# A planned single-core mixer layer: new projection order, longer holds for side matmuls, later landing times, and ScalarE as a second engine for three scalings

## The chip, the cores and the metric

The kernel runs on one core of a Trainium2 chip. The metric is the device time of one execution in microseconds (us); the median of several executions counts. The core has a matrix engine (TensorE, PE in the profile), a vector engine (VectorE, DVE), an activation engine (ScalarE, ACT), GpSimd (POOL), and queues that start transfers (DMA), nearly all of them here on SyncE (SP).

## The reference

One layer of a streaming encoder, with D = 2048 channels and 512 frames. Two groups of heads read the same projection of the input, RWKV-7 (8 pairs of heads of 64 channels) and HGRN2 (8 heads of 128 channels). Their gated results go through one output projection and a LayerNorm.

```python
proj = einsum('btd,dc->btc', x, w_in)                 # 2048 -> 8320 columns
rw, hg = token_shift(proj[..., :4224], mu), proj[..., 4224:]
r, k, v, z, wd, ad = split(rw)                        # RWKV-7
decay = exp(-exp(-softplus(-(w0 + tanh(wd) @ w_up)) - 0.5))
a = sigmoid(a0 + ad @ a_up)
kk = normalized(k * k_k);  k = k * (1 + (a - 1) * k_a)
S = S * decay + (S @ -kk) (kk * a)^T + v k^T;  o = S r    # per frame and head
o_rwkv = (groupnorm(o) + sum(r * k * r_k) * v) * silu(z)
q, f, i, g = split(hg)                                # HGRN2
f' = lb + (1 - lb) * sigmoid(f);  k' = (1 - lb) * sigmoid(-f)
S = S * f' + k' i^T;  o = silu(q) S                       # per frame and head
o_hgrn = rmsnorm(o) * g_norm_w * silu(g)
y = concat(o_rwkv, o_hgrn) @ w_out
out = layer_norm(2**0.25 * x + y, ln_w, ln_b)
```

## The kernel before

**Main matmuls.** Every fp32 operand of a projection is split into a high and a low part (`split`, one ScalarE copy and one VectorE subtraction per 128x512 part), and a product is three matmuls: high by high, high by low, low by high (`three`, L524 in the profile). The input projection is a list of units, `ORDER`: `k3` is the key projection of RWKV head pair 3, `f6` the forget gate of HGRN head 6, and so on. A unit is 48 such matmuls of 128x512 (an `i` unit 192). `ORDER` also sets the layout of the weights in memory. The output projection follows: one quarter of the columns directly (`rows`), half of them by seven Strassen products of 8 blocks, the last quarter directly, with the LayerNorm at the end.

**Side matmuls.** The recurrences run in chunks between the main matmuls. Each head pair gets ready after its `k` and `r` (`rwkv_prep`), is transposed through DRAM (`rwkv_turn`, which waits for `v`), its 64x64 systems are inverted (`rwkv_invert`, two batches of 32x32 matmuls per two pairs) and folded (`folded`, two batches of 64x64), then a scan of 8 chunks with whole-array 128x128 fp32 matmuls (`rwkv_scan`), outputs, group norm, the gate. HGRN heads go in twos (`hgrn_heads`, `hgrn_out`). Matmuls with fewer than 128 rows or columns are called narrow, 128x128 fp32 ones whole; a stretch of side matmuls between two main ones is a visit.

**The planner.** The program is written out once, by a planner (`Plan`) that keeps a clock for every engine. Every piece of side work is a generator in a queue; after each main matmul `pump` issues what fits. An instruction's place in its engine's stream is thus fixed when the program is made, by costs written in the source; the chip then only obeys semaphores. What matters here:

- `three` adds n/2400 + 0.0145 us per main matmul to PE's clock, and `TURN` = 0.215 us at each change between whole-array and narrow modes.
- `worth`: a side matmul that is ready waits until another queue has one of its kind (whole or narrow) ready as well, or until `HOLD` is over (0.3 us for whole, 1.0 for narrow). This doesn't hold in the last six projections (`HURRY`), nor when PE is already on a visit. `BURST` limits narrow matmuls to 68 in 3 us.
- `step`: a PE instruction is issued only if its operands are ready 0.35 us before now (`LEAD`); another engine's when it can start soon.
- `fetched`: a load is taken to land at its transfer time (bytes at 360 GB/s) + 1.8 us after SP's clock; `send` adds 0.44 us to SP's clock, and does not look at whether the source or the destination is ready. SP executes its transfers in order: one that waits holds back those behind it.
- `Op` has one or more engines that could do it; `best` takes the one that would end first. `ts` (a scale, or a scale and an offset per channel) has VectorE alone.

The steps that the change touches: `gates` (two scalings per HGRN head), `rwkv_prep` (the key factor `a`), `put_gated` (a finished gated block is written to DRAM, and its partner is read back for sums that Strassen needs), `reload` (gated blocks read back for the output projection), `load` (weights), `finish_last` and `row_last` with its helper `biased` (the last 128 rows: eight matmuls without a use stand between the bias product and the mean product).

Of the kernel before, what the change touches and what calls it, by code (L numbers as in the profile page):

```python
# [10 lines left out]
AF = mybir.ActivationFunctionType  # L11
ALU = mybir.AluOpType
# [4 lines left out]
T = 512  # L17
# [14 lines left out]
HALF = 1024  # L32
# [7 lines left out]
ORDER = (  # L40
# [3 lines left out]


ORDER = (
# [3 lines left out]


def _order():

    return [(u[0], int(u[1:])) for u in ORDER.split()]
# [10 lines left out]
class Plan:  # L65
# [4 lines left out]

    AFTER = {"pe": 0.2, "act": 0.145, "dve": 0.13, "pool": 0.06, "dma": 0.0, None: 0.1}
    TO_PE = 0.12
    HOLD = {"whole": 0.3, "narrow": 1.0}
    TURN = 0.215
    REST = 1.5
    LEAD = -0.35
# [81 lines left out]
            self.short.pop(0)  # L158
        return not self.short or len(self.short) + n <= self.BURST

    def fetched(self, tile, size):

        self.clock["dma"] = max(self.clock["dma"], self.clock["sp"]) + size * 128 / 360e3
        self.ready[tile.tensor.name] = (self.clock["dma"] + 1.8, "dma")

    def queue(self):
        self.queues.append([])
# [95 lines left out]
def mixer_kernel(ctx, tc, head, x_r, w_all, par, up, ln_wb, consts, hmask, out):  # L263
    nc = tc.nc
    pe, sc_e, dve, pool = nc.tensor, nc.scalar, nc.vector, nc.gpsimd
# [17 lines left out]
    plan = Plan({**BUFS, **PBUFS})  # L283
# [26 lines left out]
    def room(**need):  # L310

        return lambda: all(plan.free(tag, n) for tag, n in need.items())
# [17 lines left out]
    def send(o, i, cost=0.44):  # L330

        nc.sync.dma_start(o, i)  # L332
        plan.clock["sp"] = max(plan.clock["sp"], plan.clock["pe"]) + cost


    def size(ap):
        n = 1
        for s in ap.shape[1:]:
            n *= s
        return n  # L340
# [23 lines left out]
    def act_way(o, i, f, scale=1.0, bias=0.0):  # L364
        cost = 0.09 + size(o) * 0.00085 + moved(o, i) + (0.06 if isinstance(scale, bass.AP) else 0.0)
        if f == AF.Copy:
            return "act", cost, lambda: sc_e.activation(o, i, f, scale=scale)  # L367
        return "act", cost, lambda: sc_e.activation(o, i, f, scale=scale, bias=bias)  # L368
# [4 lines left out]
    def dve_op(reads, o, f, n=None, per=0.00104, base=0.07):  # L373
        return Op([("dve", base + (n or size(o)) * per, f)], reads, [o])
# [5 lines left out]
    def banked(ap):  # L380

        return 0.00104 if ap.tensor.name in plan.banks else 0.00076

    def ts(o, a, s1, s2, f1, f2=None):
        if f2 is None:
            return dve_op([a], o, lambda: dve.tensor_scalar(o, a, s1, None, f1), per=banked(a))
        return dve_op([a], o, lambda: dve.tensor_scalar(o, a, s1, s2, f1, f2), per=banked(a))

    def stt(o, a, s, b, f1, f2):
        return dve_op([a, b], o, lambda: dve.scalar_tensor_tensor(o, a, s, b, f1, f2), per=0.00113,  # L390
# [72 lines left out]
    nhead = 2 * FIRST  # L463
# [21 lines left out]
    def load(j):  # L485
        if j < nload:
            if j < joint or (j - joint) % 4 < 2:
                t = st("wr", [P, HALF])
                raws[j] = [t[:, :QT], t[:, QT:]]
                send(t, source(j))  # L490
                plan.fetched(t, 4 * HALF)
            else:
                raws[j] = third[(j - joint) % 4 - 2]
                for i, t in enumerate(raws[j]):
                    send(t, source(j)[:, i * QT : i * QT + QT])
                    plan.fetched(t, 4 * QT)
# [22 lines left out]
    def three(ps, lh, ll, rh, rl, first, last):  # L519
        n = size(rh)  # L520
        for i, (l, r) in enumerate(((lh, rh), (lh, rl), (ll, rh))):
            plan.clock["pe"] += n / 2400 + 0.0145 + plan.turn(("main",))
            plan.mode = ("main",)
            pe.matmul(ps, l, r, start=first and i == 0, stop=last and i == 2)  # L524
            plan.pump()
        if last:
            plan.ready[ps.tensor.name] = plan.busy[ps.tensor.name] = (plan.clock["pe"], "pe")
# [85 lines left out]
    olb, lbm = lw[:, 4], lw[:, 5]  # L613

    HW0, HA0, HKA, HRK, HGW, HGB, HHW, HOKA = range(8)

    def hcol(i, p):

        return half[:, i, p : p + 1]
# [53 lines left out]
    gated = [None] * KT  # L673
# [3 lines left out]
    spilled, stored = {}, []  # L677
# [10 lines left out]
    def put_gated(k, g):  # L688

        gated[k] = g  # L690
        if k in SPILL:
            def run():
                yield lambda: by_now(g)
                send(spill[SPILL.index(k)], g)
                now = spilled[k] = plan.clock["sp"]
                n = korder.index(k)
                m, other = n // 2, korder[n ^ 1]
                if other in spilled:
                    yield room(t=1)
                    r = take("t")  # L700
                    send(r, spill[SPILL.index(other)])
                    plan.fetched(r, 4 * T)
                    yield lambda: plan.clock["pe"] > now + 4.5
                    r1, r2 = (r, g) if n % 2 else (g, r)
                    yield from token_sums(r1, r2, r1, r2)
                    for i, r_ in enumerate((r1, r2)):
                        yield lambda: by_now(r_) and plan.clock["sp"] <= plan.clock["pe"] + 0.2
                        send(sums_a[m, i], r_)
                    stored.append(m)
                    drop(r)  # L710
                drop(g)

            plan.add(stores, run())
# [31 lines left out]
    def rwkv_prep(S, p):  # L745
# [7 lines left out]
        a, sg, kx2 = take("t"), take("t"), take("t")  # L753
# [55 lines left out]
        yield tt(ar[:, :, :C], chunks(kap), pf[:, :, :C])  # L809
        yield stt(kap, a, 1.0, kap, ALU.add, ALU.mult)  # L810
        yield stt(bk[:, :, :C], chunks(kap), 0.5, chunks(pinv), ALU.mult, ALU.mult)
        yield ts(a, a, hcol(HKA, p), hcol(HOKA, p), ALU.mult, ALU.add)
        yield tt(k, k, a)
        yield tt(bk[:, :, C:], chunks(k), chunks(pinv))
        drop(a, kap, pinv)
# [480 lines left out]
    def gates(ps, h, put):  # L1296

        def run():
            yield evac_room(2)
            f, k = take("t"), take("t")  # L1300
            yield act(f, ps, AF.Sigmoid)
            yield act(k, ps, AF.Sigmoid, scale=-1.0)
            drop(ps)
            yield ts(f, f, olb[:, h : h + 1], lbm[:, h : h + 1], ALU.mult, ALU.add)
            yield ts(k, k, olb[:, h : h + 1], None, ALU.mult)
            put(f, k)

        plan.add(evacs, run())
# [137 lines left out]
    def reload(n):  # L1446
        while len(asked) < min(n, KT):
            k = korder[len(asked)]
            asked.append(k)
            if k in SPILL:  # L1450
                plan.until(lambda: gated[k] is not None and (plan.free("t") or plan.free("g")))
                gated[k] = take("t" if plan.free("t") else "g")
                send(gated[k], spill[SPILL.index(k)])
                plan.fetched(gated[k], 4 * T)

    def split_gated(n):
        while len(whole) < min(n, KT):
# [483 lines left out]
    def row_last(t, d, ps, halves):  # L1941

        y, k = place(t, d)

        def run():
            yield lambda: (t, d) in xrs
            xr = xrs[t, d]
            yield keyed(stt(y, xr, ALPHA, ps, ALU.mult, ALU.add), [xr.tensor.name, ps.tensor.name], k + [y.tensor.name])
            drop(ps, xr)
            for i in range(2):  # L1950
                yield lambda: len(halves) > i
                c = slice(i * T // 2, i * T // 2 + T // 2)
                kc = y_keys(t, d * T + c.start, d * T + c.stop)
                yc, pc = y[:, c], halves[i]

                def weigh():
                    w = lnw[0][:, 0, d * T + c.start : d * T + c.stop]
                    yield keyed(tt(yc, yc, w), kc, kc)

                yield keyed(tt(yc, yc, pc, ALU.add), kc + [pc.tensor.name], kc)  # L1960
                yield keyed(Op([("dve", 0.07 + T // 2 * 0.00105,
                                 lambda: dve.bn_stats(stats[:, t, d + i], yc))], [], []), kc, [f"stat{t}"])
                if i == 1:

                    yield room(mix=2)
                    pbs = {e: take("mix") for e in (2, 3)}
                    plan.add(scans[1], biased(pbs))
                    yield from finish_last(t, pbs, weigh)
                    return
                yield from weigh()  # L1970

        def biased(pbs):
            for e in (2, 3):
                yield mm(pbs[e], ident, columns(t, e)[2], stop=False)
            warm = take("main" if plan.free("main") else "mix")
            for _ in range(8):
                pe.matmul(warm, gh[0][:, :P], gl[0])
                plan.clock["pe"] += 0.2275
            drop(warm)

        plan.add(sums, run())
# [132 lines left out]
```

## Time and profile before

| | us |
|---|---|
| three runs | 1018.35, 1015.20, 1016.61 |
| median | 1016.61 |
| the profiled execution | 1017.52 |
| its span, first to last instruction | 1015.7 |
| first main matmul of the output projection | 829.7 |
| VectorE busy | 864.3 |
| ScalarE busy | 507.5 |

The profiled execution is 0.9 us above the median; 1.8 us of it lie outside the span. The page gives busy time by engine; PE's is nearly the whole span because the matmuls overlap in the pipeline, so it doesn't tell how much of it is waiting. That is read from three other views: the table of waits, the chain of work that ended last (each step with what released it), and the timeline (instructions by start). There a row has the start, the time taken, the engine, the line and the tiles, written <- read, and a count. L377 is the line of `tt`, L390 of `stt`, L386 and L387 of `ts`, L367 and L368 of ScalarE's `act_way`, L353 of `mm`, L332 of `send`, L1977 of the matmuls without a use.

### The profile page before, as it was taken

What the parts mean: (1) busy time and instruction counts of PE and PEld (TensorE: products, weight loads), DVE (VectorE), ACT (ScalarE), POOL (GpSimd) and SP (SyncE); (2) the same over time, 40 slices, a digit from 0 to 9 for tenths busy, and PEclk for the clock granted to TensorE, in tenths of its full rate; (3) what the DMA queues carried; (4) which work ended last, traced back from release to release, by engine and by line L of the source; (5) the groups of instructions that cost most, each with busy time, mean ns of one, the idle gap of its engine ahead of it and who ended that gap; (6) DMA issues with size and microseconds to landing.
All of it is one profiled execution on the core that took longest, in us unless ns stands there. A gap on an engine that the chain in (4) does not pass through costs nothing.

```text
span 1015.7 us, 18890 instructions
## 1 busy us (share of the span) xinstructions
PE 1006.4 (99%) x7084; PEld 831.5 (82%) x7084; DVE 864.3 (85%) x1894; ACT 507.5 (50%) x963; POOL 43.0 (4%) x78
## 2 busy tenths in 40 slices
PE   9999999999999999999999999999999999999998
PEld 8888888888888888888887788888888878888886
DVE  7688689967898998888979987888999887998867
ACT  6557335344647335535563355736443555466531
POOL 0000000000010001002000010020001001000001
PEclk9999999999999999999999999999999999999999
DMA  9666664443446453235554432246463248797633
GB/s 348 234 208 212 228 209 146 125 136 92 133 145 182 113 147 94 65 100 152 148 181 153 107 96 84 89 130 172 136 190 114 82 136 243 235 319 229 204 127 125
DMA packets 80492, 161.74 MB, mean 159 GB/s; under 512 B 11408, under 2 KB 38288, under 8 KB 80400
## 3 DMA queue, kind: packets, MB, share of 16 engines
q1 hardware_dynamic: 79968, 159.61, 51.4%
q8 instruction: 56, 0.92, 0.4%
q10 hardware_dynamic: 432, 0.92, 0.2%
q14 instruction: 36, 0.29, 0.1%
HBM read 130.48 MB, written 30.02 MB: 158 GB/s over the span
## 4 chain that ended last, share of the span: by engine, by line
PE 39%; DVE 4%; DMA 4%; issue 1%; SPq 1%; ACT 1%; DVEq 0%; ACTq 0%
PE main L524 27%; PE mix L524 7%; PE mix L353 4%; DVE wl L377 1%; DMA wr<-w_all 1%; SPq L332 1%; DMA far<-ksq 1%; DMA q<-far 1%; DVE t L377 1%; PE main L353 1%; DMA t<-spill 1%; DVE xl L377 1%; DMA spill<-g 0%; DMA t<-far 0%; DMA g<-x_r 0%
## 5 line engine op out<-in xcount | busy, mean ns | idle before, releaser
L524 PE MATMUL main<-xl,wh 128*128 128x512 f32 x848 | 333.3, 393 | 0.0
L524 PE MATMUL main<-xh,wl 128*128 128x512 f32 x848 | 333.1, 393 | 0.0
L524 PE MATMUL main<-xh,wh 128*128 128x512 f32 x848 | 332.9, 393 | 0.0
L367 ACT ACTIVATE wh<-wr 128x512 fp32r<-128x512 f32 x285 | 177.7, 627 | 170.0 <-PE main L524 120.8
L377 DVE TENSOR_TENSOR wl<-wr,wh 128x512 fp32r<-128x512 f32 x285 | 194.2, 682 | 31.3 <-ACT wh L367 27.4
L524 PEld LDWEIGHTS main<-xh,wl 128*128 128x128 f32 x848 | 159.4, 188 | 32.5
L524 PEld LDWEIGHTS main<-xh,wh 128*128 128x128 f32 x848 | 159.3, 188 | 32.3
L524 PEld LDWEIGHTS main<-xl,wh 128*128 128x128 f32 x848 | 159.3, 188 | 32.3
L524 PE MATMUL main<-wl,xh 128*128 128x512 f32 x194 | 76.1, 392 | 0.2 <-DVE wl L377 0.2
L524 PE MATMUL main<-wh,xh 128*128 128x512 f32 x194 | 76.1, 393 | 0.1
L524 PE MATMUL main<-wh,xl 128*128 128x512 f32 x194 | 76.0, 392 | 0.0
L377 DVE TENSOR_TENSOR inv<-inv 128x256 f32<-128x256 f32 (+10 forms) x184 | 64.5, 355 | 11.0 <-DMA inv<-w_all 7.5
L524 PEld LDWEIGHTS main<-wh,xh 128*128 128x128 f32 x194 | 36.4, 188 | 8.1 <-DVE t L390 0.5
L524 PEld LDWEIGHTS main<-wl,xh 128*128 128x128 f32 x194 | 36.4, 188 | 8.1 <-DVE wl L377 0.6
L524 PEld LDWEIGHTS main<-wh,xl 128*128 128x128 f32 x194 | 36.4, 188 | 7.3
L377 DVE TENSOR_TENSOR inv<-inv,inv 64x30 f32<-64x30 f32 (+14 forms) x120 | 38.5, 320 | 2.7
L367 ACT ACTIVATE t<-mix 64x128 f32<-64x128 f32 (+3 forms) x71 | 18.4, 262 | 41.3 <-DVE zz L377 23.9
L377 DVE TENSOR_TENSOR t<-t,tot 128x256 f32<-128x256 f32 x96 | 37.9, 417 | 0.3
L368 ACT ACTIVATE t<-main,om 128x512 f32<-128x512 f32 x33 | 22.2, 685 | 29.5 <-PE main L524 22.3
L390 DVE SCALAR_TENSOR_TENSOR bd<-mix,pc,bd 64x64 f32<-64x64 f32 x112 | 31.6, 283 | 5.3 <-PE mix L353 3.0
L367 ACT ACTIVATE q<-t 128x256 f32<-128x256 f32 (+1 forms) x51 | 21.8, 445 | 25.0 <-DVE t L377 21.5
L390 DVE SCALAR_TENSOR_TENSOR t<-main,pr,t 128x511 f32<-128x511 f32 x33 | 24.3, 745 | 6.6 <-ACT t L368 6.3
(320 smaller groups left out, 1609.6 us busy)
## 6 DMA issues: line engine op xcount, KB each, us to landing
wr<-w_all SPq DMA_DIRECT2D x142, 512.0 KB, 3.9
inv<-w_all SPq DMA_DIRECT2D x16, 512.0 KB, 4.9
sums_w<-inv SPq DMA_DIRECT2D x16, 512.0 KB, 5.0
q<-head SPq DMA_DIRECT2D x14, 448.0 KB, 5.6
far<-ksq SPq DMA_DIRECT2D x22, 256.0 KB, 3.5
t<-w_all SPq DMA_DIRECT2D x20, 256.0 KB, 4.1
t<-spill SPq DMA_DIRECT2D x17, 256.0 KB, 4.4
far<-q SPq DMA_DIRECT2D x8, 512.0 KB, 5.0
```

The source lines that it names most:

```text
L332: nc.sync.dma_start(o, i)
L353: return Op([("pe", cost, lambda: pe.matmul(o, l, r, start=start, stop=stop, **kw))], [l, r], [o], mode=("narrow", l.shape[0], 32 if m <= ...
L367: return "act", cost, lambda: sc_e.activation(o, i, f, scale=scale)
L368: return "act", cost, lambda: sc_e.activation(o, i, f, scale=scale, bias=bias)
L377: return dve_op([a, b], o, lambda: dve.tensor_tensor(o, a, b, f), base=base or 0.16 if o.shape[0] < P and size(o) == C and o.tensor.name i ...
L390: return dve_op([a, b], o, lambda: dve.scalar_tensor_tensor(o, a, s, b, f1, f2), per=0.00113, base=0.085 if o.shape[0] == P and size(o) > ...
L524: pe.matmul(ps, l, r, start=first and i == 0, stop=last and i == 2)
```

## The change

1. `ORDER` is another list (twice; the second replaces the first). `k0 r0 w0` still come first; in the last third `k6 k7 v6 z5 r6` come earlier, `v7` is sixth from the end instead of ninth.
2. `HOLD` is 0.6 us for whole matmuls, 4.0 for narrow ones.
3. `three` adds 0.09 us to PE's clock after a visit that ended in whole mode.
4. `send` lets SP's clock wait for destination and source (each + 0.1 us); weight loads are taken to land 1.0 us later (2.8), gated blocks 1.5 us later (3.3); `put_gated` reads the partner back only 5 us after its write was sent.
5. `affine`, with ScalarE or VectorE, replaces `ts` at three scalings.
6. Five matmuls without a use instead of eight.

```diff
+ORDER = (
+    "w0 k0 r0 q0 r1 k1 v0 v1 g1 q1 f0 f1 k2 g0 i0 z0 f2 r3 r2 z1 "
+    "k3 f3 q3 v2 v4 q2 g3 v3 k4 q5 z3 z2 q4 r4 k5 f4 g2 v5 r5 f5 "
+    "i1 k6 k7 v6 z5 r6 g4 r7 z4 q6 f7 f6 g5 v7 q7 g7 g6 z6 z7")
...
-    HOLD = {"whole": 0.3, "narrow": 1.0}
+    HOLD = {"whole": 0.6, "narrow": 4.0}
...
-    def fetched(self, tile, size):
+    def fetched(self, tile, size, late=1.8):
...
-        self.ready[tile.tensor.name] = (self.clock["dma"] + 1.8, "dma")
+        self.ready[tile.tensor.name] = (self.clock["dma"] + late, "dma")
...
-        plan.clock["sp"] = max(plan.clock["sp"], plan.clock["pe"]) + cost
+        (to, _), (at, by) = (d.get(ap.tensor.name, (0.0, None)) for d, ap in ((plan.busy, o), (plan.ready, i)))
+        plan.clock["sp"] = max(plan.clock["sp"], plan.clock["pe"], to + 0.1, at + 0.1) + cost
...
+    def affine(o, a, s1, s2=0.0):
+
+        if isinstance(s2, float):
+            f = lambda: dve.tensor_scalar(o, a, s1, None, ALU.mult)
+            w = act_way(o, a, AF.Copy, s1)
+        else:
+            f = lambda: dve.tensor_scalar(o, a, s1, s2, ALU.mult, ALU.add)
+            w = act_way(o, a, AF.Identity, s1, s2)
+        return Op([w, ("dve", 0.07 + size(o) * banked(a), f)], [a], [o])
...
-                plan.fetched(t, 4 * HALF)
+                plan.fetched(t, 4 * HALF, 2.8 if j >= nhead + 2 else 1.8)
...
-            plan.clock["pe"] += n / 2400 + 0.0145 + plan.turn(("main",))
+            plan.clock["pe"] += n / 2400 + 0.0145 + plan.turn(("main",)) + (0.09 if plan.mode[0] == "whole" else 0.0)
...
                 if other in spilled:
+                    yield lambda: plan.clock["pe"] > spilled[other] + 5.0
...
-        yield ts(a, a, hcol(HKA, p), hcol(HOKA, p), ALU.mult, ALU.add)
+        yield affine(a, a, hcol(HKA, p), hcol(HOKA, p))
...
-            yield ts(f, f, olb[:, h : h + 1], lbm[:, h : h + 1], ALU.mult, ALU.add)
-            yield ts(k, k, olb[:, h : h + 1], None, ALU.mult)
+            yield affine(f, f, olb[:, h : h + 1], lbm[:, h : h + 1])
+            yield affine(k, k, olb[:, h : h + 1])
...
-                plan.fetched(gated[k], 4 * T)
+                plan.fetched(gated[k], 4 * T, 3.3)
...
-            for _ in range(8):
+            for _ in range(5):
                 pe.matmul(warm, gh[0][:, :P], gl[0])
```

More of the change, by code (lines that the diff above doesn't have):

```diff
@@ L49 @@
     "f5 i1 g5 k6 z4 r6 v6 k7 z5 r7 v7 q7 f7 q6 f6 g6 g7 z6 z7")
+ORDER = (
[3 rows of a table added]
+ORDER = (
[3 rows of a table added]
 def _order():
```

3 rows, old and new, of the table ORDER are left out of this document.

## The prediction

> **What bounds the kernel now.** The page's first part gives busy time by engine.
>
> ```profile
> PE 1006.4 (99%) x7084; PEld 831.5 (82%) x7084; DVE 864.3 (85%) x1894; ACT 507.5 (50%) x963; POOL 43.0 (4%) x78
> ```
>
> PE is busy all the time, but its matmuls overlap, so 99% doesn't tell what could be saved. The chain that ended last gives the pace: after its start, where the columns are start, time taken and work with a count.
>
> ```profile
> 537.77 17.94 PE main L524 x79
> ...
> 622.50 0.44 PE mix L353 x4
> ...
> 673.56 3.12 PE mix L353 x28
> ```
>
> 79 main matmuls take 17.94 us, 0.227 each. The diff changes the number of no matmul but the three without a use, so main work is a fixed sum; only PE's waits, the price of visits and the two ends can move. The waits of PE (who waited for whom, total, times, longest):
>
> ```profile
> PE mix L353 <- DVE ksq L377: 1.9, 2, 1.0
> PE mix L1339 <- DVE inv L1337: 1.1, 1, 1.1
> PE mix L353 <- DVE zz L377: 0.8, 1, 0.8
> PE main L353 <- DVE q L377: 0.5, 1, 0.5
> PE main L524 <- DVE wl L377: 0.2, 1, 0.2
> ```
>
> The row of `inv` is the first instruction of all and stays. The other four are **3.4 us in 1015.7**: all that a better schedule can win back from waiting. Three places hold them, and the chain shows what came before each:
>
> ```profile
> 522.72 4.57 DMA spill<-g
> 527.75 3.79 DMA wr<-w_all
> ...
> 536.53 0.70 DVE ksq L377
> ...
> 556.54 7.11 DMA q<-far
> ...
> 564.79 0.62 ACT q L367
> ...
> 815.44 5.20 DMA t<-spill
> 820.72 0.64 ACT xh L367
> ```
>
> At 522.7 a gated block is written to DRAM. The read of its partner stands next on SP, which holds it until the write is done, and the weights behind it start only at 527.75; VectorE splits them late, comes late to `ksq` (536.53), and PE waits (`q` 0.5 and one `ksq`). At 556.54 a transpose through DRAM takes 7.1 us and PE waits for the other `ksq` behind it. At 815.44 a gated block is read back in 5.2 us; ScalarE and VectorE stand behind it, and PE waits for `zz`.
>
> **The change part by part.**
>
> *Landing times.* Median times from issue to landing, from the page's last part:
>
> ```profile
> wr<-w_all SPq DMA_DIRECT2D x142, 512.0 KB, 3.9
> ...
> t<-spill SPq DMA_DIRECT2D x17, 256.0 KB, 4.4
> ```
>
> The old plan reckons 0.44 + 1.46 + 1.8 = 3.7 us for weights and 0.44 + 0.73 + 1.8 = 3.0 for a block read back; the new one 4.7 and 4.5. So it no longer puts a split behind data 1.4 us too early (the 815 place), and the 5 us between write and partner's read exceed the 4.57 us that held SP at 522.7. It adds no instruction. The read moves later by at most 5 us and is covered, since its sums are wanted only by Strassen, past 881 us (row under (c)). Weights are prefetched two loads ahead; a load feeds 24 main matmuls, 24 x 0.227 = 5.4 us, so two give 10.9 against 4.7 + a split: covered, and 1 us per load if not. The slow transpose (556) gets only SP's better clock. I take the two addressed places as gone and half of the third: 0.5 + 1.0 + 0.8 + 0.2 + 0.45 go, **-2.9 us** rounded; bounds -3.4 and 0.
>
> *The new order.* Every unit and every side job stays; which meet is new. The trace cannot show it. Nearest rows: the old list, made by the same planner, left three places of about 1 us. A new list has its own; bounds 0 and +3.4, and I take one such place, **+1.0 us**, since the misjudged transfers behind two of the three are now reckoned.
>
> *Longer holds.* What a joint visit saves is read from PE's timeline: two narrow batches alone and two together.
>
> ```profile
> 146.91 0.39 PE L524 MATMUL main<-xh,wh 128*128 128x512 f32 x1
> 147.23 0.89 PE L353 MATMUL mix<-q,t 128*32 128x48 f32 x64
> ...
> 148.62 0.39 PE L524 MATMUL main<-xh,wh 128*128 128x512 f32 x1
> ```
>
> ```profile
> 212.81 0.39 PE L524 MATMUL main<-xh,wl 128*128 128x512 f32 x1
> 213.13 0.75 PE L353 MATMUL mix<-big 32*32 32x32 f32 x64
> ...
> 214.38 0.39 PE L524 MATMUL main<-xh,wl 128*128 128x512 f32 x1
> ```
>
> ```profile
> 394.11 0.39 PE L524 MATMUL main<-xh,wl 128*128 128x512 f32 x1
> 394.43 0.75 PE L353 MATMUL mix<-inv,inv 32*32 32x32 f32 x64
> 395.11 0.89 PE L353 MATMUL mix<-q,t 128*32 128x48 f32 x64
> ...
> 396.50 0.40 PE L524 MATMUL main<-xh,wl 128*128 128x512 f32 x1
> ```
>
> From the last main start before to the third after, less three paces (0.68): 1.03, 0.89 and 1.71. Together they save 1.03 + 0.89 - 1.71 = 0.21 us. By the source there are 44 narrow batches; four visits of the timeline already hold two. A 4 us hold finds partners only where another job comes within 4 us, which the new order can arrange. I take six more joint visits: **-1.3 us**; bounds 0 and -2.5 (twelve). Behind a held batch nothing waits on PE (main matmuls go on), only its own head pair, up to 3 us more per batch.
>
> *Whole visits and the 0.09 us.* The chain's rows above: 28 whole matmuls 3.12, four 0.44, so (3.12 - 0.44) / 24 = 0.112 each, and four would be 0.447 with no fixed part. A whole visit costs its matmuls and next to nothing for the return, so joining them saves **0**; whatever the search gained there in its own clock, the chip does not pay back. [...]
>
> *`affine`.* VectorE's two forms and the nearest ScalarE form of the same shape (from the views by line and by form):
>
> ```profile
> L386 DVE TENSOR_SCALAR t<-t,lw x8: 471/480/483, 101.4 to 774.4; 128x512 f32<-128x512 f32 x8
> ```
>
> ```profile
> L387 DVE TENSOR_SCALAR t<-t,lw x8: 532/540/546, 100.9 to 774.0; 128x512 f32<-128x512 f32 x8
> ```
>
> ```profile
> L368 ACT ACTIVATE t<-t,pr 128x512 f32<-128x512 f32 x8 | 5.7, 718 | 0.0
> ```
>
> If all 24 moved, VectorE would lose 8 x 0.48 + 16 x 0.54 = 12.5 us of 864 and ScalarE gain 24 x 0.72 = 17.2 on 507. Every PE wait above names VectorE, and ScalarE is half idle, so it lowers the chance of a wait, but it is on no path that sets the end: **0**, bounds -0.5 (a wait like `q`) and +0.7 (one such instruction ahead of a split). [...]
>
> *The end.* From the timeline:
>
> ```profile
> 1008.01 0.40 ACT L1700 ACTIVATE nr<-cst,mv 128x128 f32<-128x128 f32 x1 [7.79 <-DVE mv L390]
> ...
> 1008.80 0.42 PEld L353 LDWEIGHTS mix<-big,nr 128*128 128x128 f32 x2
> ...
> 1010.09 1.73 DVE L390 SCALAR_TENSOR_TENSOR inv<-inv,rs,mix 128x512 f32<-128x512 f32 x3 [0.33 <-PE mix L353]
> ```
>
> `nr` is there at 1008.41, but its weights load at 1008.80, behind eight useless matmuls; three fewer free 0.68, of which 1008.80 - 1008.41 = 0.39 can be used. VectorE, idle 0.33 for it, starts earlier: **-0.3 us**; bounds 0 and -0.4.
>
> Sum: -2.9 + 1.0 - 1.3 - 0.3 = **-3.5 us**. On the profiled execution 1017.5 - 3.5 = 1014.0; that lies 0.9 above the median of the runs, so 1016.6 - 3.5 = **1013.1**. Best ends together: -3.4 - 2.5 - 0.4 = -6.3, 1010.3.
>
> **Rivals.** *(a) One set of waits for another.* The new list meets as many late VectorE results as the old: +3.4 instead of +1.0. For it: VectorE's 85%, barely lowered. Against: misjudged transfers. -3.5 + 2.4 = -1.1: 1015.5, no change that can be measured.
>
> *(b) The clock of the plan runs slow.* Each return after a whole visit is reckoned at 0.09 us where the rows have about 0.01; a scan of 14 such visits thus drifts 1.1 us, more than the 0.35 us lead, and PE comes 0.75 us early to what VectorE makes, in four scans 3 us. Against: the lead is kept before every PE instruction, and VectorE has 15% idle to catch up. -3.5 + 3.0: 1016.1, the same. [...]
>
> *(c) The last head pair comes late: slower.* `v7` is now sixth from the end, and the turn of pair 7 cannot end without it.
>
> ```profile
> 759.90:829.66 69.76, 58.94 (x242) 43.95 (x241) 1.00 0.38 114
> ```
>
> ```profile
> 584.59 0.42 SPq L332 DMA_DIRECT2D zz<-far  x1
> ```
>
> ```profile
> 787.36 0.27 PE L353 MATMUL main<-zz,big 64*64 64x64 f32 x1
> ```
>
> The stretch (busy time with count at L524) holds the last five projections, 240 matmuls, so `v7` would be through PE near 760. Pair 5 shows what follows a `v` that was waited for: from 564.79 (above) to the second `zz<-far` at 584.59, and 4.4 us to land: 24 us. 760 + 1.5 for the evacuation + 24 = 785.5; before, the fold began at 787.36. It fits by 2 us. If the turn takes 30 us, the fold is 4 us late, and at the end
>
> ```profile
> 879.33 0.69 DVE L377 TENSOR_TENSOR xl<-g,xh 128x512 fp32r<-128x512 f32 x1
> ```
>
> ```profile
> 881.34 0.39 PE L524 MATMUL main<-wh,xh 128*128 128x512 f32 x1
> ```
>
> the last split ends at 880.0, and PE wants it at 881.34 (180 matmuls into the output projection): slack 1.3. So it decides from 2 + 1.3 us of lateness; 10 us late costs 6.7: -3.5 + 6.7 = +3.2, 1019.8.
>
> **How the numbers follow.** Forecast 0.52, (a) 0.21, (b) 0.12, (c) 0.15. A measurement can tell about 0.3%, 3.05 us, from no change. The forecast's own range is 1010.3 to 1015.0; its part below 1013.55 is 0.45, and I add 0.04 from (a) with more joint visits: faster 0.49, same 0.36 (rest of forecast, (a), (b)), slower 0.15 (c). For 8 in 10: 1010.3 to 1018.0 leaves out most of (c) and little below.
>
> **What would show it.** Right: no wait of PE over 0.5 us near a read of `spill`; fewer narrow visits, main matmul to main matmul, than the 40 of before; the `nr` weights load within 0.2 us of `nr`. Wrong: PE's waits summing over 3 us; a wait near the fold or the last `xl`; whole visits dearer than 0.112 us per matmul.

## The result and the profile after

The changed kernel takes **1026.87 us** (median of four runs, 1026.19 to 1029.14) against 1017.26 for the kernel before in the same comparison. The ratio is 1.0105, 95% interval 1.0092 to 1.0119: slower by 1%. The forecast was 1013.1 with a range up to 1018.0; both were missed. The profiled execution has a span of 1024.4 us, before 1015.7.

Where the 8.7 us of span lie can be read from the instruction starts of PE, because the main work is the same in both (3876 matmuls of 512 columns and 23 of 256 up to the last block of rows, 881.3 us at 0.2267 each and, as an estimate, half of that for the 256; the median intervals in both traces are 0.227 and 0.120). A visit is counted here with the two main matmuls after it, and without the idle time that the trace shows in it:

| us | before | after |
|---|---|---|
| up to the first main matmul of 512 columns | 4.9 | 5.0 |
| main matmuls at their pace | 881.3 | 881.3 |
| visits without idle time | 110.2 | 109.3 |
| idle time of PE | 3.3 | 10.4 |
| slow stretches of main matmuls elsewhere | 5.6 | 8.5 |
| end, from the last main matmul on | 10.4 | 10.0 |

So visits and end are shorter, as was forecast (-0.9 and -0.4), and everything else is waiting and slow stretches: **+9.9 us**. The table of waits of the changed kernel has most of it (who waited for whom, total, times, longest; L547 is `three`, L366 `mm`, L390 `tt`, L413 `stt`, L380 and L381 ScalarE's `act_way`, L344 `send`):

```profile
PE main L547 <- DVE xl L390: 3.6, 1, 3.6
PE mix L366 <- DVE ksq L390: 3.5, 4, 2.1
PE mix L366 <- issue: 2.0, 1, 2.0
PE mix L1363 <- DVE inv L1361: 1.1, 1, 1.1
PE main L547 <- DVE wl L390: 0.8, 1, 0.8
PE main L1412 <- ACT xh L380: 0.3, 1, 0.3
PE mix L366 <- DVE ksq L399: 0.2, 1, 0.2
```

These add up to 11.5 us where the rows of before have 4.5. The waits behind the two reads of `spill` (at 534 and 823) are gone; whether that is by the change that the prediction named, the experiments tell. Three larger waits stand elsewhere. Each has its own chain.

**At 142 us: sums of weights.** The chain that ended last, between 130 and 143 us (start, time taken, work):

```profile
130.65 5.02 DMA sums_w<-inv
...
135.69 4.94 DMA inv<-w_all
...
140.65 0.04 DVE inv L390
140.69 0.42 issue
141.11 0.70 DVE ksq L390
```

Two 512 KB transfers, one behind the other, take 5 us each. The plan takes such a load to land 3.7 us after SP's clock, by the figures that the prediction worked out. VectorE stands 1.33 us at the subtraction for Strassen's weight sums (140.65), and `ksq`, for which PE waits 2.1 us, starts only behind it (141.11). A second delay lies before it: ScalarE had waited 4.29 us for `q<-far`, a transpose read back, until 134.71, and VectorE behind ScalarE until 137.71. Without the loads for the sums (e6, below) the same places come at 132.82 and 135.83. So the loads cost twice, by VectorE's stand and by a `q<-far` that SP issues 2.2 us later (129.75, in e6 127.55). The page's medians of all sixteen of each, from issue to landing, say the same:

```profile
inv<-w_all SPq DMA_DIRECT2D x16, 512.0 KB, 5.2
sums_w<-inv SPq DMA_DIRECT2D x16, 512.0 KB, 4.6
```

VectorE stood just as long at these loads before; the rows are first of before, then of after, from the table of waits:

```profile
DVE inv L377 <- DMA inv<-w_all: 7.5, 5, 3.3
```

```profile
DVE inv L390 <- DMA inv<-w_all: 7.2, 4, 3.6
```

The difference is only what stood behind: in the old order nothing that PE wanted soon.

**At 598 us: no one to wait for.** PE's timeline, where a joint visit of 128 narrow matmuls runs:

```profile
596.39 0.89 PE L366 MATMUL mix<-q,t 128*32 128x48 f32 x64
597.21 0.72 PE L366 MATMUL mix<-big 32*32 32x32 f32 x61
599.88 0.25 PE L366 MATMUL mix<-big 32*32 32x32 f32 x3 [1.96 <-issue]
```

PE stops for 1.96 us three matmuls before the end of the visit, and the profile shows nothing that it waits for ("issue"). The trace's packet records have a 16 KB packet on queue 8, of the kind `instruction` on the page, at 597.24 us; the one before it is at 577.24, the next at 601.00.

**At 878 us: the last head pairs.** The chain that ended last there and then PE's timeline:

```profile
860.75 7.35 DMA far<-ksq
...
868.60 5.95 DMA wr<-w_all
...
874.57 2.91 DMA t<-far
```

```profile
873.98 0.39 PE L547 MATMUL main<-wl,xh 128*128 128x512 f32 x1
877.94 0.63 PE L547 MATMUL main<-wh,xl 128*128 128x512 f32 x1 [3.58 <-DVE xl L390]
878.37 0.63 PE L547 MATMUL main<-wh,xh 128*128 128x512 f32 x1
...
881.36 0.50 PE L547 MATMUL main<-wl,xh 128*128 128x512 f32 x1
```

And VectorE's timeline:

```profile
875.54 1.14 DVE L413 SCALAR_TENSOR_TENSOR g<-t,half,t 128x128 f32<-128x128 f32 x4 [5.54 <-DMA t<-far]
...
877.20 0.69 DVE L390 TENSOR_TENSOR xl<-t,xh 128x512 fp32r<-128x512 f32 x1
```

The four instructions that write `g` from `t` and the head's weights are the finish of one of the last two RWKV pairs, after its transpose through DRAM. VectorE stands 5.54 us at them until their `t<-far` has landed (the first was issued at 868.18, right behind the slow `far<-ksq`; the chain above goes on to the last of the pair, at 874.57), and the split `xl` of another block, which PE needs, stands behind. Before, the same instruction came at 866.76 without idle time:

```profile
866.76 1.14 DVE L390 SCALAR_TENSOR_TENSOR g<-t,half,t 128x128 f32<-128x128 f32 x4
```

While VectorE stood there, the DMA engines were busy at a share of 0.95 (columns: us, busy time with count of PE, its weight loads, VectorE, ScalarE and GpSimd, then clock, DMA share, GB/s); in the second row PE works again, at a lower clock (0.68 over this stretch, 0.50 from 878.2 to 881.5):

```profile
870.00:876.00 6.00, 4.36 (x20) 3.28 (x18) 0.46 (x3) 1.34 (x3) 0.00 (x0) 1.00 0.95 234
877.70:883.00 5.30, 5.06 (x15) 4.03 (x16) 5.30 (x12) 1.46 (x3) 0.00 (x0) 0.68 0.47 145
```

After 3.58 us without work, the eight intervals from 877.94 to 881.36 take 3.42 us, 0.427 each instead of 0.227: 1.6 us more, so this one place costs 3.7 + 1.6 = 5.3 us.

The rest are mostly stops of about 0.3 to 1.1 us in six more places (323, 574, 645, 710, 720 and 895), some 3.7 us together.

### The profile page after: what moved, and what is told of

Read it like the earlier page. It is cut to its first block, busy times and chain, and to the rows that moved or that the text cites. A ratio compares the mean times of both kernels' runs of the same rounds, so it can differ in the third digit from the quotient of the medians.

```text
span 1024.4 us, 18887 instructions
## 1 busy us (share of the span) xinstructions
PE 1007.7 (98%) x7081; PEld 831.3 (81%) x7081; DVE 860.6 (84%) x1898; ACT 513.4 (50%) x959; POOL 41.6 (4%) x78
## 4 chain that ended last, share of the span: by engine, by line
PE 87%; DMA 5%; DVE 4%; issue 1%; ACT 1%; SPq 0%; DVEq 0%; ACTq 0%
PE main L547 66%; PE mix L366 10%; PE mix L547 7%; PE main L1412 3%; PE main L366 2%; DVE wl L390 1%; DMA q<-far 1%; DMA far<-ksq 1%; DMA t<-far 1%; DVE t L390 1%; DMA wr<-w_all 1%; DVE g L413 1%; DMA q<-head 1%; DVE inv L390 1%; DMA g<-x_r 1%
## 5 line engine op out<-in xcount | busy, mean ns | idle before, releaser
L547 PE MATMUL main<-xh,wl 128*128 128x512 f32 x864 | 340.5, 394 | 0.8 <-DVE wl L390 0.8
L547 PE MATMUL main<-xh,wh 128*128 128x512 f32 x864 | 338.8, 392 | 0.1
L547 PE MATMUL main<-xl,wh 128*128 128x512 f32 x864 | 338.8, 392 | 0.0
L380 ACT ACTIVATE wh<-wr 128x512 fp32r<-128x512 f32 x285 | 177.7, 626 | 177.8 <-PE main L547 135.1
L390 DVE TENSOR_TENSOR wl<-wr,wh 128x512 fp32r<-128x512 f32 x285 | 194.1, 682 | 28.8 <-ACT wh L380 26.6
L547 PEld LDWEIGHTS main<-xh,wl 128*128 128x128 f32 x864 | 162.3, 188 | 35.0 <-DVE wl L390 1.7
L547 PEld LDWEIGHTS main<-xl,wh 128*128 128x128 f32 x864 | 162.3, 188 | 33.8
L547 PEld LDWEIGHTS main<-xh,wh 128*128 128x128 f32 x864 | 162.4, 188 | 33.1 <-ACT wh L380 0.5
L547 PE MATMUL main<-wh,xl 128*128 128x512 f32 x194 | 76.6, 395 | 3.6 <-DVE xl L390 3.6
L547 PE MATMUL main<-wh,xh 128*128 128x512 f32 x194 | 76.8, 396 | 0.0
L547 PE MATMUL main<-wl,xh 128*128 128x512 f32 x194 | 76.7, 395 | 0.0
L390 DVE TENSOR_TENSOR inv<-inv 128x256 f32<-128x256 f32 (+10 forms) x184 | 64.6, 356 | 10.7 <-DMA inv<-w_all 7.2
L547 PEld LDWEIGHTS main<-wh,xl 128*128 128x128 f32 x194 | 36.8, 190 | 11.5 <-DVE xl L390 4.0
L547 PEld LDWEIGHTS main<-wl,xh 128*128 128x128 f32 x194 | 36.9, 190 | 7.7
L547 PEld LDWEIGHTS main<-wh,xh 128*128 128x128 f32 x194 | 36.8, 189 | 7.6
L390 DVE TENSOR_TENSOR inv<-inv,inv 64x30 f32<-64x30 f32 (+14 forms) x120 | 38.6, 321 | 3.0
L381 ACT ACTIVATE t<-main,om 128x512 f32<-128x512 f32 x33 | 22.3, 687 | 37.2 <-PE main L547 30.0
L413 DVE SCALAR_TENSOR_TENSOR bd<-mix,pc,bd 64x64 f32<-64x64 f32 x112 | 31.7, 283 | 7.1 <-PE mix L366 4.6
L390 DVE TENSOR_TENSOR t<-t,tot 128x256 f32<-128x256 f32 x96 | 36.9, 417 | 0.2
L380 ACT ACTIVATE q<-t 128x256 f32<-128x256 f32 (+1 forms) x55 | 23.2, 442 | 23.6 <-DVE t L390 21.7
L381 ACT ACTIVATE t<-main 128x512 f32<-128x512 f32 x32 | 18.5, 594 | 31.2 <-PE main L547 28.8
L380 ACT ACTIVATE t<-mix 64x128 f32<-64x128 f32 (+3 forms) x61 | 15.8, 261 | 33.3 <-DVE zz L390 21.0
```

Of the source, the lines that this page charges most:

```text
L390: return dve_op([a, b], o, lambda: dve.tensor_tensor(o, a, b, f), base=base or 0.16 if o.shape[0] < P and size(o) == C and o.tensor.name i ...
```

## The experiments

All ratios are to the kernel before on the same chip, with the 95% interval in brackets; times are medians.

**e1 and e2: list or settings.** The diff's list and its settings were swapped one at a time. e1 is the changed kernel with the old list:

```diff
-    "w0 k0 r0 q0 r1 k1 v0 v1 g1 q1 f0 f1 k2 g0 i0 z0 f2 r3 r2 z1 "
...
+    "w0 k0 r0 q1 k1 r1 v1 f1 q0 v0 f0 g0 g1 i0 z0 z1 r3 k2 f2 r2 "
+    "k3 q2 v2 f3 v3 r4 z2 q3 g3 q5 g2 k4 v4 z3 g4 k5 f4 r5 q4 v5 "
+    "f5 i1 g5 k6 z4 r6 v6 k7 z5 r7 v7 q7 f7 q6 f6 g6 g7 z6 z7")
```

> The changed kernel with the list of projections of before; holds, landing times, the 0.09 us, the three scalings and the end as changed. Theory A (the new list is what costs; the other parts help): 1012 to 1017 us, PE's waits under 3 us. Rival B (the planner's new settings cost, whatever the list): 1022 us or more, with waits of PE of 8 us and more again.

Measured: **1086.68**, 1.0697 (1.0680 to 1.0715). The largest row of its table of waits:

```profile
PE main L547 <- ACT xh L380: 16.2, 1, 16.2
```

Side work is put off until no projection is left to cover it: the fold of the last two pairs begins at 887.0 us, in the kernel before at 787.4, and PE waits in the output projection (this row at 943).

e2 is the kernel before with the new list and nothing else.

> The kernel before with the new list alone. Theory A: as slow as the changed kernel, 1022 to 1030 us, waits of PE of 8 us and more. Rival B: within 4 us of before, 1013 to 1021.

Measured: **1026.11**, 1.0097 (1.0082 to 1.0112): the whole loss, with the list alone changed. Its largest row:

```profile
PE mix L353 <- DVE ksq L377: 3.5, 2, 3.0
```

The 3.0 is near the same place (134 us), but here ScalarE stands 7.07 us for `q<-far`, issued behind an `inv<-w_all` of 6.57 us and VectorE's work on it; VectorE itself stands at no sum by then. The waits at 598 and 878 are absent or small (0.6), and others are in their place, 2.0 us at 485 the largest. No wait is left at 534 or 823, though the landing times are the old ones. So settings 2 to 6 together are worth about nothing on the new list (1.0105 with them, 1.0097 without), and they decide which waits there are more than how much waiting.

**e3 and e4: one suspected cause moved.** e3 lets the LayerNorm's weights be fetched only after all gated blocks are split, out of the crowd at 870.

```diff
     def fetch_norm():
+        yield lambda: len(whole) == KT
         yield room(big=1)
```

> The changed kernel, where the LayerNorm weights (4 x 512 KB) are fetched only after all gated blocks are split. Theory (those loads crowd the transfers between 862 and 877, so a weight load and a transpose land late, PE waits 3.7 us for xl and then runs nine matmuls at half clock): the wait and the half clock go, -4 to -5.5 us, 1021 to 1023. Rival (the last head pair is late by itself): the wait stays above 2 us and the time within 1.5 us of the changed kernel's 1026.9.

Measured: 1028.41, 1.0125 (1.0108 to 1.0142), a miss. The wait at 878 is gone. Another one stands 20 us later, where SP now has two of the moved loads (887.63 and 895.39) among the reads for the output projection:

```profile
897.46 0.50 PE L547 MATMUL mix<-wl,xh 128*128 128x512 f32 x1 [2.51 <-DVE wl L390]
```

VectorE's stand at `t<-far` is 2.98 us there instead of 5.54. Main matmul for main matmul, e3 is 4.5 us behind the changed kernel at 870, though the order on PE is the same throughout and on VectorE up to 869; it wins 5.5 us back between 870 and 882 and loses 2.7 between 890 and 950. So the forecast gain is there at its place, and the total, with lateness from elsewhere in it, doesn't show it.

e4 puts 24 more PE instructions ahead of the kernel: if the 16 KB packets of queue 8 are PE's instructions, the visits move against them.

```diff
-    for _ in range(WARM):
+    for _ in range(WARM - 6):
         pe.matmul(warm, zero, zero)
+    for _ in range(12):
+        pe.matmul(warm[:, :64], zero, zero[:, :64])
```

> The changed kernel, where the warm-up matmuls at the very start are cut into smaller ones, so that PE's instruction stream has 24 more instructions (weight loads and matmuls) ahead of all else and no more time. Theory (the 2.0 us gap at 597.9 inside a joint visit is PE's instruction fetch: a block of 256 is asked for in the burst and comes 2 us too late): the gap of 2 us at about 598 goes, -2 us unless another visit now meets a block's edge. Rival (it is a semaphore or memory effect of that visit): the gap stays at the same matmul.

Measured: 1030.73, 1.0144 (1.0124 to 1.0164). The joint visit now runs through:

```profile
602.91 0.89 PE L366 MATMUL mix<-q,t 128*32 128x48 f32 x64
603.73 0.75 PE L366 MATMUL mix<-big 32*32 32x32 f32 x64
```

The gap is won back there: main matmul for main matmul, e4's lag behind the changed kernel falls from 6.5 to 4.4 us between 588 and 635. But 2.8 were lost at the start and 2.6 near 134 to 146, so the total says nothing of it. Nor does e4 show that the shift did it: in e3, with as many recorded PE instructions ahead of this visit as in the changed kernel (8134) and no shift, the visit runs through as well, and the lag falls from 6.0 to 3.8.

**e5: the changed kernel again,** to see how firm its waits are.

> The changed kernel once more, as the measure for the runs beside it. 1026 to 1029 us. PE's waits near 134 to 146 us and near 878 come again (same program); the 2.0 us gap inside the joint visit near 598 comes again if it hangs on the program alone, and stays away if it hangs on how a transfer of instructions happens to run.

Measured: 1029.17, 1.0127 (1.0100 to 1.0154), with waits at the same instructions (142, 323, 598, 710 and 878 of the changed kernel); the one at 710 is 2.0 us here instead of 0.8. They belong to the program, not to one execution, though their sizes move.

**e6, e7 and their controls e13, e14: the loads left out.** The loads that e3 moved made a new wait (2.51 us at 897); so here loads were taken away. e6 leaves out 14 of the 16 loads of weights for Strassen's sums, e7 also the four loads of the LayerNorm's weights; the sums are then made of stale data, and the LayerNorm's weights are set to 1. SP's clock in the plan goes on as if the loads were sent, and the traces show PE, VectorE and ScalarE with the same instructions in the same order as in the changed kernel.

```diff
-            send(w, w_all[nsent + i].rearrange("p (a c) -> p a c", a=4))
+            if i < 2:
+                send(w, w_all[nsent + i].rearrange("p (a c) -> p a c", a=4))
+            else:
+                plan.clock["sp"] = max(plan.clock["sp"], plan.clock["pe"], plan.busy.get(w.tensor.name, (0.0, None))[0] + 0.1) + 0.44
...
-            send(w[:, :, c], ln_wb[None, :, c].to_broadcast([P, 2, T]))
+            if d == 0:
+                pool.memset(w, 1.0)
+            (to, _) = plan.busy.get(w.tensor.name, (0.0, None))
+            plan.clock["sp"] = max(plan.clock["sp"], plan.clock["pe"], to + 0.1) + 0.44
```

> The changed kernel, same order of instructions, where 14 of the 16 loads of output weights for Strassen's weight sums are left out (the sums are then made of stale data). Theory (VectorE stands in its sums for such a load, 5 to 8 us each, and what PE needs at 134 to 146 is behind it): those waits go, 2.5 to 4 us less than the changed kernel beside it. Rival (the new list leaves PE without its transposes there anyway): less than 1 us.

> As the run before, and the LayerNorm weights (2 MB read, 848 to 866 us) are not loaded either but set to 1. Theory (those loads hold up a weight load and a transpose, so PE waits 3.7 us for xl near 878 and then runs nine matmuls at half clock): a further 4 to 5.5 us less, with no new wait near 897. Rival (late by itself): less than 1.5 us.

Measured: **1023.82**, 1.0072 (1.0055 to 1.0089), and **1021.51**, 1.0051 (1.0035 to 1.0068). The rows of e6 and then of e7:

```profile
PE main L547 <- DVE xl L390: 3.6, 1, 3.6
PE mix L366 <- DVE ksq L390: 1.9, 3, 0.9
PE mix L366 <- issue: 1.8, 1, 1.8
```

```profile
PE mix L366 <- issue: 2.3, 1, 2.3
PE mix L366 <- DVE ksq L390: 1.2, 3, 0.7
```

First the long `ksq` wait goes, then the `xl` wait as well, with VectorE's stand at `t<-far` down to 2.18 us:

```profile
871.49 1.14 DVE L413 SCALAR_TENSOR_TENSOR g<-t,half,t 128x128 f32<-128x128 f32 x4 [2.18 <-DMA t<-far]
```

The gap at 598 stays in both. The step from e6 to e7 is within the two intervals, so its size rests on the trace.

e13 and e14 leave the same loads out of the kernel before; the order on PE, VectorE and ScalarE is again unchanged.

> Control for e6: the kernel before with the same 14 of 16 weight-sum loads left out, order of instructions unchanged. Left out: the weights' sums for the Strassen products are made of stale tiles, so the output is not the layer's. The changed kernel lost 5.4 us by it (1029.2 to 1023.8). Theory A (the late sum loads cost time only where the new list puts work of TensorE behind them): the kernel before stays within 1.5 us of itself, 1015 to 1018.5. Theory B (these transfers cost every list as much, so e6 said nothing of the list): 1010 to 1013.

> Control for e7: the kernel before without 14 of 16 weight-sum loads and without the four loads of the LayerNorm's weights (set to 1), both left out of the computation. Theory A: within 1.5 us of the kernel before, 1015 to 1018.5, so that e7's 7.7 us were a cost of the new list. Theory B: 1007 to 1012.

Measured: **1016.42**, 1.0000 (0.9990 to 1.0009), and **1015.94**, 0.9995 (0.9986 to 1.0005). The old order pays nothing for these transfers. So they are no cost of their own; they cost in the new order, where PE's work stands behind them. Of the 1.27% that the changed kernel loses in e5, 0.76 points go with them.

**e8 and e9: the holds.** e8 is the changed kernel with the old `HOLD`, e9 has the old list as well.

```diff
-    HOLD = {"whole": 0.6, "narrow": 4.0}
+    HOLD = {"whole": 0.3, "narrow": 1.0}
```

> The changed kernel with the old holds (0.3 and 1.0 us). Theory (the list costs, not the holds): within 4 us of the changed kernel beside it, and about as many waits elsewhere. Rival (longer holds make the last heads late): the wait near 878 is gone and the time is 4 us or more lower.

> The changed kernel with the list of before and the holds of before; the rest as changed. Theory C (the long holds are what made the old list take 1086.7 us, since side work is put off and piles up at the output projection): 1014 to 1025 us and no wait of PE over 3 us. Rival (the landing times or the 0.09 us did it): above 1040.

Measured: 1027.22, 1.0118 (1.0094 to 1.0142), and 1027.46, 1.0105 (1.0085 to 1.0126), one round for e9. On the new list the longer holds are worth nothing that the medians show. Narrow visits are 41 instead of 37 and the gap at 598 is gone, but the two largest waits lie near the old places again, 2.7 us at 135 and 1.9 at 877, the second behind another tile:

```profile
PE mix L366 <- DVE ksq L390: 4.6, 3, 2.7
PE mix L371 <- DVE t L390: 1.9, 1, 1.9
```

On the old list they cost about 60 us (1.0697 less 1.0105), by the late recurrences that e1 shows; that 4 us of waiting per batch are how it comes is argued only, and e11 below comes apart alike with the old holds. e9 still stands 1% above the kernel before, with the old list, the old holds and the remaining settings: the loss doesn't need the new list. It also keeps a wait behind a read of `spill`, 1.4 us at 532.5 after 0.9 at 526.9, with the new landing times and the 5 us in place:

```profile
514.15 4.87 DMA spill<-g
...
519.09 6.61 DMA t<-spill
...
531.63 0.69 DVE ksq L390
```

**e10: the end alone,** five useless matmuls instead of eight in the kernel before.

> The kernel before with five matmuls without a use instead of eight. Theory: the nr weights load 0.4 us earlier, -0.3 us, which the intervals cannot tell from nothing; the profile shows the load within 0.2 us of nr. Rival: no earlier load, as nr itself is late.

Measured: 1016.32, 0.9999 (0.9991 to 1.0008). The timeline of e10:

```profile
1006.54 0.40 ACT L1700 ACTIVATE nr<-cst,mv 128x128 f32<-128x128 f32 x1 [7.80 <-DVE mv L390]
1007.00 0.30 PEld L353 LDWEIGHTS mix<-big,nr 128*128 128x128 f32 x2 [0.40 <-ACT nr L1700]
```

`nr` is there at 1006.94, its weights load 0.06 us later. From the start of `nr` to VectorE's last group (1008.21) it is 1.67 us, before 2.08: the 0.4 us are won at their place, and too small for the medians.

**e11, e12 and e15: the landing figures.** e11 is the kernel before (with e10's end) with the loads for weight sums taken to land 2.2 us later:

```diff
             plan.fetched(w, 4 * HALF)
+            plan.ready[w.tensor.name] = (plan.clock["dma"] + 4.0, "dma")
```

e12 is the changed kernel with the same 2.2 us, and 1.0 us more for the stores of the sums. e15 is the changed kernel with the old landing times, the old clock of SP and no 5 us between write and partner's read.

> The kernel before with five matmuls at the end, and the loads of the weight sums taken to land 2.2 us later (4.0 after the transfer time), so that VectorE is not put behind a load that isn't there. Theory: VectorE's idle time for inv<-w_all falls from 7.5 us to under 2; PE had no wait behind it in this kernel, so 1014 to 1017 us, same as before. Rival (any new placement gives new waits): 1018 to 1026.

> The changed kernel with the loads of the weight sums taken to land 2.2 us later and their stores 1.0 us later. Theory (those two figures of the plan are what the wait near 142 comes from): no PE wait of over 1 us between 110 and 200 us; -2 to -3 us there, while later waits come out anew, 1020 to 1029 in all. Rival: the wait near 142 stays.

> Changed kernel, with the old landing times, the old clock of SP and without the 5 us between write and partner's read; new list and other settings stay. Theory A (the landing figures only choose where the waits fall): 1024 to 1032, with a wait of TensorE behind a weight split or a read of spill that the changed kernel doesn't have. Theory B (the list was searched with its figures and comes apart without them, as the old list did): over 1040, main matmuls ahead before the output projection and far behind at its end.

Measured: e11 **1081.08**, 1.0631 (1.0617 to 1.0646); e12 1028.27, 1.0110 (1.0094 to 1.0126); e15 1027.31, 1.0101 (1.0080 to 1.0121). In e11 the figure does what it says, VectorE's stand at these loads falls from 7.5 to 2.0 us, and yet the plan comes apart as in e1:

```profile
PE main L524 <- ACT xh L367: 16.1, 1, 16.1
```

In e12 the waits at 134 to 146 are gone, and a new one takes their place at 498, 6.9 us for `wl`.

In the profiled execution of e15, the quickest of its four (1023.57), no wait is over 1.7 us and all add up to 9.1; the median is as in the changed kernel. Its trace also shows how little the landing figures do here: up to 780 us PE, VectorE and ScalarE have the same instructions in the same order as in the changed kernel, and only the order of the transfers differs, from 322 us on. Better transfer times for the plan, taken singly, bought nothing.

**e16: the scalings on ScalarE,** in the kernel before.

```diff
-        yield ts(a, a, hcol(HKA, p), hcol(HOKA, p), ALU.mult, ALU.add)
+        yield affine(a, a, hcol(HKA, p), hcol(HOKA, p))
...
-            yield ts(k, k, olb[:, h : h + 1], None, ALU.mult)
+            yield affine(k, k, olb[:, h : h + 1])
```

> Kernel before with the three scalings free to go to ScalarE; old list and all else unchanged. Prediction's term: 0, bounds -0.5 and +0.7, so 1016 to 1018. Theory B (any figure changed under a list that was tuned without it makes side work pile up at the end): over 1030.

Measured: **1021.38**, 1.0048 (1.0033 to 1.0063), between the two theories. Its table of waits has ten where before has six, eight of them under 1 us, and adds up to 7.5 us where before has 4.5; that is 3.0 of the 5.1 us, and the rest isn't worked out.

The 0.09 us of `three` was not tried by itself.

## Why the prediction was wrong

- **The step that failed: "A new list has its own; bounds 0 and +3.4, and I take one such place, +1.0 us".** The bounds were taken from the old list, and the changed kernel has +9.9 us of waits and slow stretches. e2 shows the list alone to cost 0.97%, 9.9 us of 1016, and the whole change costs 1.05%. The fault is in the sample: the old list's waits were the only row at hand, and they are not typical. Nor is it this list alone: e9 costs 1.05% with the old list. Two of the prediction's own signs of being wrong came, waits over 3 us (11.5) and one at the last `xl`. Every kernel here whose plan differs from the one of before in more than the last instructions lies between 1.0048 and 1.0697; the three that keep its order (e10, e13, e14) lie between 0.9995 and 1.0000.
- **Where the waits come from** was only half seen. The prediction read late transfers near `spill`. The same kind of lateness stood in the trace of before in VectorE's own waits, 7.5 us for `inv<-w_all`, which cost PE nothing there. e6 with e13, and e7 with e14, show these loads to cost the new order about 0.55 and 0.2 points and the old none. A wait of an engine that PE doesn't feel is not slack that the next order keeps.
- **Landing times: waits removed (-2.9)** failed as well. No chain of a wait of the changed kernel has a read of `spill` as its last transfer (the wait at 323 stands beside such a read, but its chain goes back to a `t<-far` that landed at 316.32). The figures aren't the reason: e2 and e15, with the old ones, have no wait at 534 or 823 either, and e9, with the new ones on the old list, still waits 0.9 and 1.4 us behind the read at 519. The sign that the prediction had set for itself, no such wait, was met for another reason.
- **Longer holds (-1.3).** Mechanism right: narrow visits, main matmul to main matmul, are 37, and 41 on the same list with the old holds (e8), where the visits take 111.0 us instead of 109.3. Against the kernel before, with 40, the visits win 0.9. The cost that was held against them, "only its own head pair", was wrong in general: on the old list they cost about 60 us.
- **The end (-0.3).** Right; it gave 0.4 (e10), in the changed kernel too: `nr` is ready at 1017.47 and its weights load at 1017.52. **Whole visits (0)** were not tried by themselves; four whole matmuls in the changed kernel's chain still take 0.45 us (at 642.90), as in the prediction's rows.
- **`affine` (0, at most +0.7).** On the old list it costs 5.1 us (e16). The prediction weighed the instructions and not the new plan that they cause (PE has the order of before only up to 72 us), the same fault as with the list.
- **Rival (c), the last head pair late,** was nearest to what happened. The fold of the last two pairs begins at 796.36, before at 787.36, and their finish crosses busy DMA engines (a share of 0.95 from 870 to 876); VectorE stands at it, with a split behind. It cost 5.3 us against the 6.7 worked out for it. But it isn't the whole loss: e3 has no such wait and e8 one of 1.9 us, and both take the same time. Rival (a), one set of waits for another, had the right form with a third of the size; (b) is not supported, since e2 without the 0.09 us loses as much.
- **Still open:** e7 stays 0.51% above the kernel before. Its table of waits adds up to 7.2 us, that of e14 to 3.4; of this difference of 3.8 us the gap at 598 is 2.3, and the rest are small waits behind VectorE's queue (571, 709, 854 and 890, 0.6 to 0.9 each), none of which was taken away by itself. Their medians are 5.6 us apart, so nearly 2 us are in no wait.

No kernel here beats the kernel before; e10 equals it.

## What to carry to other kernels

Where the order of every engine is written out ahead by a plan, a list and the plan's figures are one thing: changing one under the other can move every wait, so don't size "new waits" by those that the old order has left. How late the transfers really land against the plan (here 5 us against 3.7), and how much of it is hidden now, would be the better start, though no run here tries it as a forecast. Before a reorder, list the waits of the feeding engines too: what they hide is what the new order may uncover. And when a load is suspected, take it out of both kernels; what only the new one wins is the order's cost, and where a load is merely moved, read the place and not the total, since the move can make new waits (2.51 us in e3).

## What was not expected of the hardware

- **PE stopped inside a dense visit where the profile names nothing that it waited for.** 128 narrow matmuls, 256 instructions with their weight loads, take 1.6 us when they run through (e3, e4). In five executions (the changed kernel, e5, e6, e7, e15) PE stops 1.6 to 2.3 us in this visit, each time three matmuls before its end. Queue 8, of the kind `instruction` on the page, has 56 packets of 16 KB, 0.92 MB in all; PE's 14306 recorded instructions would be some 256 for each. In these five a packet starts 0.7 to 1.5 us after the visit does, and the next follows 3.5 to 3.8 us later. In e3 and e4 the visit runs through, and the packet lies 4.0 and 6.8 us ahead of it. So the stop goes with a packet that starts inside the visit. That these packets are PE's instructions, and that PE waits for them, as the theory of e4 has it, is the author's estimate from these numbers, and no run shows it; why the packet comes earlier in e3, where nothing was shifted, stays open.
- **3.6 us without work cost a further 1.6.** The granted clock in the stretch after the wait at 878 is 0.68, and 0.50 from 878.2 to 881.5; matmuls come every 0.427 us for 3.4 us, instead of every 0.227. After the shorter stops of this execution, 2.14 us at 142 and 1.96 at 598, it is 1.00. What sets the clock is not shown.
